# A token mixer's local kernels, made in four strips of 32 output partitions

## The chip, the cores and the metric

The kernel runs on one core of one Trainium2 chip. The metric is the device time of one execution in microseconds (us). Three runs of the kernel before gave a median of 2519.0 us, from 2516.42 to 2520.09.

## The reference

A two-layer decoder step over 272 prompt rows (16 meta tokens and 256 tokens) and 32 sample rows, width 2048, in fp32. Layer 0 is a gated short convolution and an MLP (2048 to 8192 to 2048, squared ReLU). Layer 1 is an S5 mixer and an MLP; a final norm closes it.

The S5 mixer has 128 groups of 16 channels, each with 64 complex states. Per group `g` it computes `h[t] = abar*h[t-1] + bbar u[t]` and `y[t] = Re(C h[t]) + D u[t]`, with `abar` and `bbar` made from the weights (`lambda`, `log_step`, `B`). The kernel works on four time steps at once: within a block of four, `y` gets a lower-triangular set of small matrices, the local kernels `K[g][tau] = Re(C abar^tau bbar)` (16 x 16 for tau = 0 to 3), with `D` added on the diagonal of tau = 0; what comes from earlier blocks goes through the state.

## The kernel before

**The weight stream.** All big matrices are read in slots of 256 rows by 512 columns (512 KB). SyncE issues the slots' DMAs (line 55) into four raw buffers; ScalarE makes a rounded copy `whi` (L66), VectorE the rest `wlo` (L68), three buffers of each. `WeightStream.take` makes the split two slots ahead of the one in use, and issues the DMAs for up to four slots beyond these. One slot is one *step* of `group`: 24 matmuls (L196 to L198: `whi` by high part, `whi` by low part, `wlo` by high part). Four PSUM tiles of seven belong to a group of steps; their evictions (L735 to L736, L797, L839 to L841) are put in between the matmuls on VectorE and ScalarE.

**The background list.** The S5 mixer's coefficients don't depend on the activations. They are computed during the first MLP by the list `bg`, one entry per step at the end of the step (a generator takes several steps, `None` is a step without work):

```python
            if bg:
                f = bg[0]
                ...
                        it = f()
```

Nothing but this list orders the entries against the steps. On GpSimd, which has little else to do there, they run in the order of the list as soon as what they wait for is done.

**The part that is changed.** `t_a4` turns two tables and `D` from [group, ...] to [..., group] by transposes into one PSUM tile `px` (there is one such buffer) and copies `D` as [16 channels, 128 groups]. `t_kalloc` writes zeros over the DRAM tensor `d_t` (2 MB). `t_kload(c)` loads B and C tables for 16 groups, `t_kmm(c, part)` multiplies eight groups (contraction over 128 state rows, 16 output channels by 4 x 16 columns each) into PSUM partitions 0 to 15, and ScalarE copies the result (16 x 512) into `ks`, a [16 channels, 128 groups, 4, 16] area in SBUF. `t_d` adds `D` with two GpSimd operations over 16 partitions by 2048 elements (L699, L701), and `t_tout(j)` stores from there to `d_t` the 4-j taps of input row j, one DMA of GpSimd's queue for each of four j (L704). The list after that is empty, and GpSimd's next instruction is the clearing of the S5 mixer's work area (L887), which reuses the same memory. The mixer reads `d_t` much later (`load_t`).

Of the kernel before, what the change touches and what calls it, by code (L numbers as in the profile page):

```python
# [11 lines left out]
AF = mybir.ActivationFunctionType  # L12
ALU = mybir.AluOpType
# [3 lines left out]
P = 128  # L17
# [62 lines left out]
def build(ctx, tc, I, O, dbg=None):  # L80
    nc = tc.nc
    V, S, G, T = nc.vector, nc.scalar, nc.gpsimd, nc.tensor
# [9 lines left out]
    def psum():  # L92
        return pp.tile([P, 512], F32, tag="ps", name="ps", bufs=7)

    def psum1():
        return pp.tile([P, 512], F32, tag="px", name="px", bufs=1)
# [61 lines left out]
    pend = []  # L158
# [77 lines left out]
    ident = cp.tile([P, P], F32, name="ident")  # L236
# [31 lines left out]
    big = rp.tile([P, 12000], F32, tag="BIG", name="big")  # L268
# [176 lines left out]
    d_t = dp.tile([4, 16, P, 4, 16], F32, name="d_t")  # L445

    def prep_tasks():
        L = []
        st = {}
# [7 lines left out]
        def nat(i, n=64):  # L457
            return st["vy"][:, i * 64:i * 64 + n]
# [101 lines left out]
        def t_a4():  # L560
            ps = psum1()
            for ri in range(2):
                T.transpose(out=ps[:64, ri * P:(ri + 1) * P], in_=nat(14 + ri), identity=ident)
            T.transpose(out=ps[:16, 256:256 + P], in_=nat(30, 16), identity=ident)
            V.tensor_copy(out=nat(28, P)[:16], in_=ps[:16, 256:256 + P])
            for g2 in range(2):
                sl = slice(g2 * 64, g2 * 64 + 64)
                re = ps[:64, 0:P].rearrange("p (q g) -> p q g", g=2)[:, :, g2]
                im = ps[:64, P:2 * P].rearrange("p (q g) -> p q g", g=2)[:, :, g2]
                V.tensor_copy(out=a4[sl, 0, :], in_=re)  # L570
                V.tensor_copy(out=a4[sl, 1, :], in_=re)
                V.tensor_scalar(out=a4[sl, 2, :], in0=im, scalar1=-1.0, scalar2=None, op0=ALU.mult)
                V.tensor_copy(out=a4[sl, 3, :], in_=im)
# [98 lines left out]
        def kld(c):  # L672
            off = (c % 2) * 1280
            b = st["big"]
            return (b[:, off:off + 256].rearrange("r (g c) -> r g c", g=16),
                    b[:, off + 256:off + 1280].rearrange("r (g x) -> r g x", g=16))

        def t_kload(c):
            wl, cl = kld(c)
            gs = slice(c * 16, c * 16 + 16)  # L680
            G.dma_start(out=wl, in_=d_b.rearrange("r p g c -> (r p) g c")[:, gs, :])
            G.dma_start(out=cl, in_=d_c.rearrange("r p g t c -> (r p) g (t c)")[:, gs, :])

        def ks():
            return st["big"][:16, 2560:2560 + 8192].rearrange("r (g t e) -> r g t e", t=4, e=16)

        def t_kmm(c, part):
            wl, cl = kld(c)
            ps = psum1()
            for g in range(part * 8, part * 8 + 8):  # L690
                T.matmul(out=ps[:16, g % 8 * 64:(g % 8 + 1) * 64], lhsT=wl[:, g, :], rhs=cl[:, g, :],
                         start=True, stop=True)
            g0 = c * 16 + part * 8
            pend.append(lambda: S.activation(out=ks()[:, g0:g0 + 8].rearrange("r g t e -> r (g t e)"), in_=ps[:16, :512],
                                             func=AF.Copy))

        def t_d():
            tmp = st["big"][:16, 0:2048].rearrange("r (g e) -> r g e", e=16)
            G.tensor_tensor(out=tmp, in0=ident[:16, :16].unsqueeze(1).to_broadcast([16, P, 16]),  # L699
                            in1=nat(28, P)[:16].unsqueeze(2).to_broadcast([16, P, 16]), op=ALU.mult)  # L700
            G.tensor_tensor(out=ks()[:, :, 0, :], in0=ks()[:, :, 0, :], in1=tmp, op=ALU.add)  # L701

        def t_tout(j):
            G.dma_start(out=d_t[j, :, :, j:4, :].rearrange("c g i e -> c g (i e)"),  # L704
                        in_=ks()[:, :, 0:4 - j, :].rearrange("c g t e -> c g (t e)"))

        L.append(t_kalloc)
        L += [lambda: t_kload(0), lambda: t_kload(1)]
        L += [None] * 12
        for c in range(8):  # L710
            for part in range(2):
                L.append(lambda c=c, part=part: t_kmm(c, part))
            if c < 6:
                L.append(lambda c=c: t_kload(c + 2))
            L += [None] * 4
        L += [t_d, None]
        for j in range(4):
            L += [lambda j=j: t_tout(j), None]
# [9 lines left out]
    def rhs_of(x):  # L728
        return lambda kt: (x[:, 0, kt, :], x[:, 1, kt, :])

    def rhs_hid(b):
        return lambda kt: (b[kt // 8][:, 0, kt % 8, :], b[kt // 8][:, 1, kt % 8, :])
# [42 lines left out]
    for mg in range(4):  # L775
        for part in range(3):
            if mg == 0 and part == 0:
                later(rstd_conv, 7)
            ps = group(KALL, rhs_of(xs), N0, fast=mg == 0 and part == 0)
            if mg % 2 == 0 and part == 2:  # L780
                z[mg // 2] = rp.tile([P, 2, 8, N0], F32R, tag="HID", name="z", bufs=2)
            for i in range(4):
                t = mg * 4 + i
# [40 lines left out]
    for mg in range(4):  # L824
        ps = group(KALL, rhs_hid(z), N0)
# [267 lines left out]
    def advance(n):  # L1093

        for _ in range(n):
            next(scan1, None)
# [76 lines left out]
    heavy[0] = False  # L1173
    W.limit = end0
    bg += [None] * BGOFF + prep_tasks()
    mlp(lambda: xs_mlp, N0, MLP, ssm_pre)
    assert not bg
# [4 lines left out]
    ps = psum()  # L1182
# [54 lines left out]
    part = ssm["part"]  # L1237
# [15 lines left out]
    for gi in range(NPHASE1):  # L1253
        ps = group(K1, rhs_g, N1, 0, each=lambda: advance(PUNITS))
# [55 lines left out]
    for gi, (n, mg) in enumerate(glu):  # L1310
# [3 lines left out]
        ps = group(K2 if gi < NPHASE1 else KALL, rhs_g, N1)  # L1314
# [33 lines left out]
    for mg in range(4):  # L1348
        for j in range(4):
            ps = psum()  # L1350
            for i in range(4):
                t = mg * 4 + i
                T.transpose(out=ps[:NL, i * P:(i + 1) * P], in_=xf[:, t * N1 + j * NL:t * N1 + (j + 1) * NL], identity=ident)  # L1353
            dst = ov[:, j, mg * 512:(mg + 1) * 512]
# [34 lines left out]
```

## Time and profile before

| | |
|---|---|
| median of three runs | 2519.0 us (2516.42 to 2520.09) |
| the profiled execution's own time | 2517.89 us |
| its span, first to last instruction | 2516.1 us |
| TensorE (PE) busy | 2448.6 us, 97% |
| VectorE (DVE), ScalarE (ACT), GpSimd (POOL) busy | 59%, 39%, 8% |
[...]
| DMA traffic | 418.17 MB, 166 GB/s |

1.8 us of the profiled execution's time lie outside its span. Matmuls are pipelined: a matmul of a step is recorded with 0.30 us, but they start about 0.14 us apart, so time lost on TensorE is read from the starts and from marked idle times, not from the busy share.

### The profile page before, as it was taken

The page shows a single profiled execution, that of the slowest core. Times are in us where ns is not written, and L with a number is a line of the kernel's source. Part 1 is how long each engine was busy: PE and PEld are TensorE (multiplying, and loading weights), DVE is VectorE, ACT ScalarE, POOL GpSimd, SP SyncE. Part 2 cuts the span into 40 slices and gives each one's busy share as a digit, 9 for nine tenths or more (in the row PEclk, how much of TensorE's full clock was granted, in tenths as well). Part 3 has the DMA queues.
Part 4 walks back from the last instruction along what each step waited for, and adds up shares of the span by engine and source line. Part 5 has one row for each costly group of instructions (what it writes and reads, how often), then busy time and mean ns, then how long its engine had stood idle before and what let it go on. Part 6 is the DMA issues. An engine that isn't in the chain of part 4 may idle for free. (4 is left out here: it accounts for less than half of the span.)

```text
span 2516.1 us, 43317 instructions
## 1 busy us (share of the span) xinstructions
PE 2448.6 (97%) x18078; PEld 2427.3 (96%) x18078; DVE 1477.3 (59%) x2123; ACT 974.2 (39%) x1235; POOL 189.0 (8%) x325
## 2 busy tenths in 40 slices
PE   6999999999999999999999889999999999999998
PEld 6999999999999999999998789999999999999998
DVE  5644555678565776554546964656555555545555
ACT  4333334433443333333324534443333333333334
POOL 2000000000010122000234022000000000000000
PEclk9999999999999999999999999999999999999999
DMA  6555555556666677655569544555555555555553
GB/s 153 156 157 158 158 159 175 156 158 162 191 172 206 184 218 221 192 168 169 138 167 179 149 126 144 167 163 166 168 167 163 167 165 169 161 169 166 167 168 105
DMA packets 256353, 418.17 MB, mean 166 GB/s; under 512 B 64484, under 2 KB 68260, under 8 KB 255980
## 3 DMA queue, kind: packets, MB, share of 16 engines
q1 hardware_dynamic: 248448, 389.62, 52.5%
q0 software_dynamic: 7648, 25.73, 4.9%
q8 instruction: 142, 2.33, 0.4%
q14 instruction: 55, 0.45, 0.1%
q10 hardware_dynamic: 60, 0.05, 0.0%
HBM read 392.71 MB, written 22.63 MB: 165 GB/s over the span
## 5 line engine op out<-in xcount | busy, mean ns | idle before, releaser
L68 DVE TENSOR_TENSOR wlo<-raw,whi 128x1024 fp32r<-128x1024 f32 x701 | 862.0, 1230 | 888.5 <-ACT whi L66 886.2
L66 ACT ACTIVATE whi<-raw 128x1024 fp32r<-128x1024 f32 x704 | 743.5, 1057 | 1015.0 <-PE ps L197 874.9
L196 PE MATMUL ps<-hid,whi 128*128 128x304 f32 (+1 forms) x2048 | 612.0, 299 | 11.7 <-DVE h L797 11.7
L197 PE MATMUL ps<-hid,whi 128*128 128x304 f32 (+1 forms) x2048 | 611.8, 299 | 0.0
L198 PE MATMUL ps<-xs_m,wlo 128*128 128x304 f32 (+1 forms) x2048 | 610.8, 298 | 0.1
L198 PE MATMUL ps<-hid,wlo 128*128 128x304 f32 (+1 forms) x2048 | 610.9, 298 | 0.0
L197 PE MATMUL ps<-xs_m,whi 128*128 128x304 f32 (+1 forms) x2048 | 610.2, 298 | 0.0
L196 PE MATMUL ps<-xs_m,whi 128*128 128x304 f32 (+1 forms) x2048 | 610.1, 298 | 0.0
L196 PEld LDWEIGHTS ps<-hid,whi 128*128 128x128 f32 x2048 | 385.8, 188 | 13.4 <-DVE h L797 12.7
L198 PEld LDWEIGHTS ps<-hid,wlo 128*128 128x128 f32 x2048 | 386.6, 189 | 0.0
L197 PEld LDWEIGHTS ps<-hid,whi 128*128 128x128 f32 x2048 | 385.8, 188 | 0.0
L196 PEld LDWEIGHTS ps<-xs_m,whi 128*128 128x128 f32 x2048 | 384.6, 188 | 1.1
L198 PEld LDWEIGHTS ps<-xs_m,wlo 128*128 128x128 f32 x2048 | 384.7, 188 | 0.4 <-DVE wlo L68 0.4
L197 PEld LDWEIGHTS ps<-xs_m,whi 128*128 128x128 f32 x2048 | 384.5, 188 | 0.1
L196 PE MATMUL ps<-xs,whi 128*128 128x304 f32 x768 | 233.7, 304 | 3.5 <-DVE h L388 3.5
L198 PE MATMUL ps<-xs,wlo 128*128 128x304 f32 x768 | 233.4, 304 | 0.0
L197 PE MATMUL ps<-xs,whi 128*128 128x304 f32 x768 | 232.9, 303 | 0.0
L735 ACT ACTIVATE hid<-at 128x304 fp32r<-128x304 f32 (+1 forms) x128 | 57.8, 452 | 293.0 <-DVE at L841 293.0
L198 PE MATMUL ps<-g,wlo 128*128 128x288 f32 x512 | 151.1, 295 | 0.0
L196 PE MATMUL ps<-g,whi 128*128 128x288 f32 x512 | 151.1, 295 | 0.0
L197 PE MATMUL ps<-g,whi 128*128 128x288 f32 x512 | 150.7, 294 | 0.0
L196 PEld LDWEIGHTS ps<-xs,whi 128*128 128x128 f32 x768 | 145.9, 190 | 3.8 <-DVE h L388 3.7
(283 smaller groups left out, 2337.9 us busy)
## 6 DMA issues: line engine op xcount, KB each, us to landing
raw<-in_mlp_w_up SPq DMA_DIRECT2D x256, 512.0 KB, 3.7
raw<-in_mlp_w_down SPq DMA_DIRECT2D x256, 512.0 KB, 3.7
raw<-in_conv_w_in SPq DMA_DIRECT2D x96, 512.0 KB, 3.7
raw<-in_conv_w_out SPq DMA_DIRECT2D x32, 512.0 KB, 3.6
raw<-in_ssm_glu_w_b SPq DMA_DIRECT2D x32, 512.0 KB, 3.7
raw<-in_ssm_glu_w_a SPq DMA_DIRECT2D x32, 512.0 KB, 3.5
ssm_big<-d_m SPq DMA_DIRECT2D x64, 128.0 KB, 3.4
d_m<-prep POOLq DMA_DIRECT2D x16, 256.0 KB, 9.4
```

Of the source, the lines that this page charges most:

```text
L66: self.nc.scalar.activation(out=hi, in_=r, func=AF.Copy)
L68: eng.tensor_tensor(out=lo, in0=r, in1=hi.bitcast(F32), op=ALU.subtract)
L196: T.matmul(out=o, lhsT=wh, rhs=xh, start=si == 0 and kk == 0, stop=False)
L197: T.matmul(out=o, lhsT=wh, rhs=xl, start=False, stop=False)
L198: T.matmul(out=o, lhsT=wl, rhs=xh, start=False, stop=si + 2 >= len(kts) and kk == 1)
L735: S.activation(out=dh, in_=src, func=AF.Copy)
```

## The change

`t_kmm` handles all 16 groups of a `t_kload` in one call. Group `g = 4x + s` of the sixteen goes to PSUM partitions 32x to 32x + 31 (four strips), columns 64s to 64s + 63. Its stationary operand is read 32 columns wide: its own 16 and the following 16, whose rows of output nobody uses. One ScalarE copy (128 x 256) then serves 16 groups. `ks` becomes [128, 32 x 4 x 16], in which a strip holds 16 channels of every fourth run of four groups. `t_d` works on 128 partitions by 512 elements; for this `t_a4` brings `D` into the strips with four small matmuls against the identity, each followed by a VectorE copy of the strip's columns and a copy of a 16 x 16 identity (before: one transpose, one copy). `t_tout(j)` issues four DMAs, one per strip, so sixteen instead of four. The number of entries in the list is unchanged: where the second call of `t_kmm` stood is a `None`.

```diff
-            T.transpose(out=ps[:16, 256:256 + P], in_=nat(30, 16), identity=ident)
-            V.tensor_copy(out=nat(28, P)[:16], in_=ps[:16, 256:256 + P])
+            V.memset(nat(28, P), 0.0)
+            for x in range(4):
+                sl = slice(32 * x, 32 * x + 16)
+                T.matmul(out=ps[sl, 256:256 + P], lhsT=nat(30, 16), rhs=ident, start=True, stop=True)
+                V.tensor_copy(out=nat(28, 32)[sl].rearrange("r (c s) -> r c s", s=4),
+                              in_=ps[sl, 256:256 + P].rearrange("r (c x s) -> r c x s", x=4, s=4)[:, :, x, :])
+                V.tensor_copy(out=nat(29, 16)[sl], in_=ident[sl, sl])
...
-            return st["big"][:16, 2560:2560 + 8192].rearrange("r (g t e) -> r g t e", t=4, e=16)
+            return st["big"][:, 2560:2560 + 2048].rearrange("r (g t e) -> r g t e", t=4, e=16)
...
-        def t_kmm(c, part):
+        def t_kmm(c):
             wl, cl = kld(c)
+            wf = st["big"][:, (c % 2) * 1280:(c % 2) * 1280 + 272]
             ps = psum1()
-            for g in range(part * 8, part * 8 + 8):
-                T.matmul(out=ps[:16, g % 8 * 64:(g % 8 + 1) * 64], lhsT=wl[:, g, :], rhs=cl[:, g, :],
-                         start=True, stop=True)
-            g0 = c * 16 + part * 8
-            pend.append(lambda: S.activation(out=ks()[:, g0:g0 + 8].rearrange("r g t e -> r (g t e)"), in_=ps[:16, :512],
-                                             func=AF.Copy))
+            for s_ in range(4):
+                for x in range(4):
+                    g = x * 4 + s_
+                    T.matmul(out=ps[32 * x:32 * x + 32, s_ * 64:(s_ + 1) * 64], lhsT=wf[:, g * 16:g * 16 + 32],
+                             rhs=cl[:, g, :], start=True, stop=True)
+            pend.append(lambda: S.activation(out=ks()[:, c * 4:c * 4 + 4].rearrange("r g t e -> r (g t e)"),
+                                             in_=ps[:, :256], func=AF.Copy))
 
         def t_d():
-            tmp = st["big"][:16, 0:2048].rearrange("r (g e) -> r g e", e=16)
-            G.tensor_tensor(out=tmp, in0=ident[:16, :16].unsqueeze(1).to_broadcast([16, P, 16]),
-                            in1=nat(28, P)[:16].unsqueeze(2).to_broadcast([16, P, 16]), op=ALU.mult)
+            tmp = st["big"][:, 0:512].rearrange("r (g e) -> r g e", e=16)
+            G.tensor_tensor(out=tmp, in0=nat(29, 16).unsqueeze(1).to_broadcast([P, 32, 16]),
+                            in1=nat(28, 32).unsqueeze(2).to_broadcast([P, 32, 16]), op=ALU.mult)
             G.tensor_tensor(out=ks()[:, :, 0, :], in0=ks()[:, :, 0, :], in1=tmp, op=ALU.add)
 
         def t_tout(j):
-            G.dma_start(out=d_t[j, :, :, j:4, :].rearrange("c g i e -> c g (i e)"),
-                        in_=ks()[:, :, 0:4 - j, :].rearrange("c g t e -> c g (t e)"))
+            dst = d_t[j].rearrange("c (k x s) i e -> c x k s (i e)", x=4, s=4)
+            for x in range(4):
+                G.dma_start(out=dst[:, x, :, :, j * 16:],
+                            in_=ks()[32 * x:32 * x + 16, :, 0:4 - j, :].rearrange("r (k s) t e -> r k s (t e)", s=4))
...
         for c in range(8):
-            for part in range(2):
-                L.append(lambda c=c, part=part: t_kmm(c, part))
+            L.append(lambda c=c: t_kmm(c))
             if c < 6:
                 L.append(lambda c=c: t_kload(c + 2))
-            L += [None] * 4
+            L += [None] * 5
```

## Rows read from the trace of the kernel before

**Rows 1.** The page's busy times: engine, us, share of the span, instructions.
```profile
PE 2448.6 (97%) x18078; PEld 2427.3 (96%) x18078; DVE 1477.3 (59%) x2123; ACT 974.2 (39%) x1235; POOL 189.0 (8%) x325
```

**Rows 2.** The chain that ended last: start, us, what. Its beginning, and after the MLP.
```profile
1254.63 17.71 DMA raw<-in_mlp_w_down
...
1273.53 1.23 DVE wlo L68
...
1337.52 3.59 DMA d_u<-h
```

**Rows 3.** TensorE in order of time, around its two stops: start, duration, [idle before].
```profile
1251.23 0.30 PE L198 MATMUL ps<-hid,wlo 128*128 128x304 f32 x1
1255.04 0.42 PE L196 MATMUL ps<-hid,whi 128*128 128x304 f32 x1 [3.51 <-DVE h L797]
...
1269.86 0.30 PE L198 MATMUL ps<-hid,wlo 128*128 128x304 f32 x1
1275.19 0.62 PE L196 MATMUL ps<-hid,whi 128*128 128x304 f32 x1 [5.04 <-DVE h L797]
```

**Rows 4.** Two stretches, tile ps alone: PE, PEld, DVE, ACT busy, PEclk, DMA.
```profile
1242.10:1280.30 38.20, 29.64 (x186) 29.16 (x187) 3.71 (x8) 0.00 (x0) 0.87 0.77 141
1285.00:1325.00 40.00, 40.00 (x291) 40.00 (x290) 5.54 (x12) 0.00 (x0) 1.00 0.61 169
```

**Rows 5.** GpSimd in order of time, 1238 to 1285 us.
```profile
1242.27 3.69 POOL L699 TENSOR_TENSOR prep<-ident,nat 16x2048 f32<-16x2048 f32 x1 [46.77 <-PE px L691]
1246.03 5.54 POOL L701 TENSOR_TENSOR prep<-prep 16x2048 f32<-16x2048 f32 x1
1251.87 0.53 POOL L704 DMA_DIRECT2D d_t<-prep  x1 [0.30 <-POOL prep L701]
...
1274.66 4.37 POOL L887 MEMSET ssm_big<- 128x5120 f32 x1 [18.40 <-DMA d_t<-prep]
```

**Rows 6.** VectorE in order of time, same stretch.
```profile
1243.79 3.26 DVE L68 TENSOR_TENSOR wlo<-raw,whi 128x1024 fp32r<-128x1024 f32 x1 [1.40 <-ACT whi L66]
...
1247.46 4.45 DVE L841 SCALAR_TENSOR_TENSOR at<-zt 128x304 f32<-128x304 f32 x1
...
1254.52 0.46 DVE L797 TENSOR_TENSOR h<-h,ps 128x304 f32<-128x304 f32 x1
```

**Rows 7.** GpSimd's DMA queue (packets, MB, share of 16 engines): 1249 to 1255, 1249 to 1277, 648 to 675 us.
```profile
q0 software_dynamic: 16, 0.52, 82.6%
...
q0 software_dynamic: 272, 1.31, 63.0%
...
q0 software_dynamic: 640, 2.10, 38.4%
```

**Rows 8.** One line's DMAs, the four stores L704 of t_tout: time to landing.
```profile
DMA to landing us min/median/max: 6.9/14.2/19.4
```

**Rows 9.** TensorE in order of time around one call of t_kmm.
```profile
1236.36 0.30 PE L198 MATMUL ps<-hid,wlo 128*128 128x304 f32 x1
1236.59 1.07 PE L691 MATMUL px<-prep 128*16 128x64 f32 x16
1237.59 0.40 PE L196 MATMUL ps<-hid,whi 128*128 128x304 f32 x1
```

**Rows 10.** One line's matmul: t_kmm's form, duration min/median/max ns, first and last start.
```profile
L691 PE MATMUL px<-prep x256: 219/219/230, 1060.1 to 1242.0; 128*16 128x64 f32 x128
```

**Rows 11.** TensorE, then VectorE, in order of time during t_a4.
```profile
594.74 0.27 PE L564 MATMUL px<-ident,nat 128*16 128x128 f32 x1
...
595.05 0.28 DVE L565 COPY nat<-px 16x128 f32<-16x128 f32 x1 [1.05 <-PE px L564]
595.26 0.20 DVE L570 COPY a<-px 64x64 f32<-64x64 f32 x1
```

**Rows 12.** GpSimd's groups by line and form: count, busy us, mean ns.
```profile
L654 POOL DMA_DIRECT2D d_m<-prep x32 | 20.0, 632 | 22.6 <-DVE prep L645 19.9 <-DMA d_c<-prep 2.4 <-issue 0.2
...
L1107 POOL TENSOR_TENSOR ssm_xr<-a,ssm_big 128x320 f32<-128x320 f32 x2 | 1.8, 886 | 0.1
```

## The prediction

> **What bounds the kernel now.** First the busy times: TensorE is busy 97% of the span, the others far less [rows 1]. So what matters is where TensorE stops, what work goes through it, and what feeds it. A step takes 24 matmuls; undisturbed, 291 matmuls of the steps start in 40.00 us, 0.137 us apart [rows 4].
>
> Next the chain that ended last. It begins at 1254.63 us, in the middle of the kernel, with a weight slot's DMA that took 17.71 us [rows 2]; behind the MLP it goes on through the stores that start the S5 mixer [rows 2]. So up to 1254 us TensorE has lost hardly anything to waits, and what is gained around there comes off the end.
>
> Then TensorE in order of time around that place. It stops twice: its matmuls start at 1251.23 and then at 1255.04, and at 1269.86 and then at 1275.19, both times until a VectorE eviction [rows 3]. In the stretch that holds both, 1242.10 to 1280.30, it started 186 matmuls at a mean granted clock of 0.87; undisturbed these take 186 x 40.00/291 = 25.6 us, and the stretch has 38.2. **12.6 us are lost there:** 3.7 + 5.2 in the two holes (each distance of starts less 0.14), and the other 3.7 in matmuls at the lower clock behind them [rows 3, 4].
>
> Last, who caused it, in the other engines' order of time. GpSimd runs the two operations of `t_d`, 3.69 and 5.54 us over 16 partitions, from 1242.27 to 1251.6 [rows 5]. In that time a VectorE subtraction L68 took 3.26 us (1.23 in the chain [rows 2]) and L841 took 4.45, where another operation of 128x304 takes 0.46 [rows 6]: VectorE was held for 2.0 + 4.0 = 6.0 us. TensorE's hole was 3.7, so about 2.3 us of lateness were covered by work done ahead. Then come the four stores: the last landed 19.4 us after its issue [rows 8], and GpSimd's clearing L887 waited 18.40 us for them [rows 5]. This is when the weight slot took 17.71 us: the second hole.
>
> **The change part by part.**
>
> *GpSimd's two operations (`t_d`).* From 2048 elements per partition to 512. A quarter of the rows is 0.92 and 1.38 us [rows 5]; by GpSimd's 128x320 multiplication, 0.886 us [rows 12], 512 elements take 1.4. So 2.3 to 2.8 us instead of 9.2. VectorE was held for 6.0 of 9.2 us; of 2.8 it is held for at most 2.8, likely 1.8, against the 2.3 us of cover: a hole of 0 to 0.5 us, and I take 0. (If VectorE's work ahead were used up just then, the loss would be the whole 1.8.) The scratch of the multiplication now lies over an earlier call's table only, so it may run some steps earlier; both operations are then apart, which helps. The first hole with its slow clock goes.
>
> *The stores (`t_tout`).* The bytes stay: 1.31 MB. The first of before was 16 packets, one of 32 KB for each DMA engine, and held all sixteen for 82.6% of 6 us, 5.0 us at 106 GB/s [rows 7]. All four held them for 63.0% of 28 us, 17.6 us in 272 packets, 17 per engine [rows 7]. The weight slot that came through in 17.71 us needs 16 packets per engine if one moves a 2 KB row: one weight packet to each packet of a store, as if the two queues took turns. This is my reading of why the slot was late: not the bytes, but long packets. The mixer's earlier stores show how short pieces are packed: 2.10 MB in 640 packets, that is eight DMAs of 16 KB per engine in 4 packets of 4 KB and a small one [rows 7]. By that, the strips' DMAs have per engine 2, 2, 1 and 1 packets of data (8, 6, 4, 2 KB for j = 0 to 3) and a small one, times four strips: 40 packets instead of 17. With the engine time unchanged at 17.6 us (16 partitions per DMA as before), and 40 weight packets of about 0.1 us between, the stores last some 21 us and let 2.5 slots pass instead of one. TensorE ran 18.0 us from the first store's issue until it was empty [rows 3, 5]. The first slot lands after 16 of 40 turns, 8 to 11 us; the split and the wait for it take 3 more: in time. The second lands at 17 to 20 us and is wanted at 18.0 + 3.3 - 3 = 18.3. I take a hole of 0.6 us, with bounds of 0 and the old 5.2 + 1.9 us (if the turns are not the cause, and the engine time alone is). GpSimd issues sixteen DMAs, 16 x 0.63 = 10 us by the nearest row [rows 12], less than the transfer, with nothing behind them but L887. L887 starts when they have landed; `t_d` begins some 3 us earlier (the last products come with the call that was the pair's first) and is 6.5 us shorter, so it starts earlier than before even if the stores last 21 us.
>
> [...]
>
> *The products (`t_kmm`).* 128 groups as before, and 256 passes (two matmul records per group). A call took 1237.59 - 1236.36 - 0.14 = 1.09 us for 16 passes [rows 9]; I put it at 16 x 0.054 + 0.22 for entering and leaving. Eight calls of 32 passes fewer by eight entries: 8 x 0.22 = **-1.8 us**. Does a stationary operand of 32 columns, written to another strip each time, keep 0.054 us a pass? The trace of before has all outputs at partition 0. Bounds: above, each pass takes the 0.219 us that one lasts from start to end [rows 10], +42 us; below, four strips run beside each other. A matmul of 304 columns comes every 0.137 us and one of 64 every 0.054, so a column costs 0.35 ns and 64 of them 0.022 us; a quarter of that saves 0.017 us x 256 = -4.4 us. I take 0.054: the records are the same kind and the pass was already mostly not columns.
>
> *ScalarE.* Eight copies of 128x256 for sixteen of 16x512: less, and ScalarE is busy 39% [rows 1]. Nothing; if the cover were gone, still a gain.
>
> *`D` into strips (`t_a4`).* One transpose goes, four small matmuls come, each into the PSUM tile that VectorE then reads. Before, no matmul follows a read of the same tile. If each waits for the copy ahead of it, a round is the matmul 0.27, hand-over 0.04, copy 0.20 [rows 11], back to TensorE 0.06 (VectorE's L797 ends at 1254.98, TensorE starts at 1255.04 [rows 3, 6]): 0.57. Three rounds and a last short matmul: **+1.8 us**. Bounds: 0.3 without waits, 3.4 with the identity's copies in the round. TensorE has nothing else in its queue to run meanwhile; the eight copies and a memset run on VectorE inside these stops, and it had waited 1.05 us for TensorE there [rows 11].
>
> [...]
>
> *Sum:* -12.6 + 0.6 - 1.8 + 1.8 = **-12.0 us**. Against the profiled execution's own 2517.9 us that is 2505.9. That execution lies 1.1 us below the median of the runs, so the median after should be some 2506 to 2507: I say **2506.5**.
>
> **The rivals.**
>
> *The stores still starve the stream.* If the DMA engines' 17.6 us count and not the length of the packets, the second hole and its clock stay in part or whole: up to 7.1 us back, 2507 to 2513; if sixteen transfers also last 3 us longer than four, 2516. For it: the same 16 partitions feed each DMA. Against: one slot in 17.7 us fits the turns.
>
> *A new wait takes the gain.* GpSimd's operations again fall on a full VectorE, or `t_a4`'s rounds are 2 us each: 5 to 8 us back, 2512 to 2516 and no change that can be told.
>
> *The strips run beside each other:* 4.4 us more, 2502. [...] Against it: a pass is mostly fixed time.
>
> *The other side: the strips drain the array.* If a change of strip costs a pass its full length, +42 us: 2548. It decides the sign from 12.0/256 = 0.047 us per pass on, and is measurably slower from 17/256 = 0.066. For it: no row with an output off partition 0. Against: the same form of matmul, pipelined to a quarter of its length.
>
> **How the numbers follow.** 0.2% of the median is 5.0 us, about what a measurement of this kernel can tell from no change: faster means below 2514, slower above 2524. Chances: forecast (2504 to 2510) 0.58; starved stream 0.18, half of it below 2514; new wait 0.08, nearly all "same"; strips beside each other 0.09; drain 0.07, nearly all slower. Faster 0.58 + 0.09 + 0.10 = 0.77, same 0.16, slower 0.07. The drain and a few per cent at the ends are left out of the range: 2501 to 2517.
>
> **What would show it.** Right: no TensorE idle above 1 us and a clock of 1.00 in the 45 us after the last product; L68 and L841 there near 1.2 and 0.5 us; no weight slot's DMA above 12 us; products at 1.9 to 2.0 us a call; the chain no longer begins with a slot of the MLP near 1250; three stops of 0.2 to 0.4 us in `t_a4`. Wrong: a hole behind the stores as before, or records of the products that don't overlap.

## The result and the profile after

The kernel after takes 2495.77 us in the median of four runs (2491.91 to 2498.42); four runs of the kernel before beside it give 2517.71 (2514.84 to 2520.09). The ratio is 0.9912, with a 95% interval of 0.9895 to 0.993: 22 us less. The prediction was 2506.5 with a range from 2501, so the sign was right and the gain was 10 us larger than said. The profiled execution took 2495.24 us, with a span of 2493.4.

The page's busy times of the kernel after, to be read beside [rows 1]:

```profile
PE 2431.8 (98%) x18085; PEld 2412.8 (97%) x18085; DVE 1473.5 (59%) x2131; ACT 968.6 (39%) x1227; POOL 189.8 (8%) x337
```

TensorE is still the engine that is nearly always busy, with 16.8 us less of busy time and some of its idle time gone. Where both come from is read by finding one and the same matmul of a step (the same slot, the same term) in both traces and comparing its start:

| the same step's matmul | before, us | after, us | after less before |
|---|---|---|---|
| behind `t_a4` | 594.77 | 597.90 | +3.1 (of it +0.7 already ahead of `t_a4`) |
| just ahead of the first product call | 1059.88 | 1063.52 | +3.6 |
| behind the last product call | 1242.11 | 1233.06 | -9.1 |
| behind the two holes | 1281.25 | 1259.67 | -21.6 |
| end of the S5 mixer | 1512.89 | 1490.28 | -22.6 |

So `t_a4` costs 2.4 us, the products give 12.7, the two holes give 12.5, and nothing else moves by more than about 1 us. (Between the profiled executions' own times, 2517.89 and 2495.24, it is 22.65.)

**`t_a4`.** TensorE in order of time in the kernel after; an idle time and its releaser stand in brackets:

```profile
595.27 0.38 PE L563 MATMUL px<-ident,nat 128*64 128x128 f32 x2
595.58 0.39 PE L568 MATMUL px<-ident,nat 128*16 128x128 f32 x2
596.24 0.39 PE L568 MATMUL px<-ident,nat 128*16 128x128 f32 x2 [0.27 <-DVE nat L569]
596.91 0.39 PE L568 MATMUL px<-ident,nat 128*16 128x128 f32 x2 [0.28 <-DVE nat L569]
597.58 0.39 PE L568 MATMUL px<-ident,nat 128*16 128x128 f32 x2 [0.28 <-DVE nat L569]
597.90 0.41 PE L196 MATMUL ps<-hid,whi 128*128 128x304 f32 x1
```

Each matmul of `D` from the second on waits for VectorE's copy out of the strip ahead of it: three stops, in rounds of 0.67 us.

**The products.** TensorE in order of time around the last call of the kernel after, beside [rows 9]:

```profile
1228.79 0.30 PE L198 MATMUL ps<-hid,wlo 128*128 128x304 f32 x1
1229.03 0.65 PE L701 MATMUL px<-prep 128*32 128x64 f32 x32
1229.61 0.41 PE L196 MATMUL ps<-hid,whi 128*128 128x304 f32 x1
```

Thirty-two passes and their call cost 1229.61 - 1228.79 - 0.14 = 0.68 us, where sixteen cost 1.09 before. One pass still lasts 219 ns from start to end, as in [rows 10]; what changed is the distance of starts, on the mean (0.65 - 0.22)/31 = 0.014 us, against (1.07 - 0.22)/15 = 0.057 before.

**The two holes.** GpSimd, then VectorE, in order of time in the kernel after, beside [rows 5, 6]:

```profile
1209.05 1.06 POOL L708 TENSOR_TENSOR prep<-nat 128x512 f32<-128x512 f32 x1 [22.84 <-PE px L701]
1230.27 1.31 POOL L710 TENSOR_TENSOR prep<-prep 128x512 f32<-128x512 f32 x1 [20.17 <-ACT prep L703]
1231.88 7.35 POOL L715 DMA_DIRECT2D d_t<-prep  x11 [0.30 <-POOL prep L710]
...
1252.01 4.39 POOL L897 MEMSET ssm_big<- 128x5120 f32 x1 [6.06 <-DMA d_t<-prep]
...
1231.11 1.55 DVE L68 TENSOR_TENSOR wlo<-raw,whi 128x1024 fp32r<-128x1024 f32 x1 [0.97 <-ACT whi L66]
...
1233.08 0.47 DVE L851 SCALAR_TENSOR_TENSOR at<-zt 128x304 f32<-128x304 f32 x1
```

The two operations of `t_d` are now 21 us apart and take 1.06 and 1.31 us instead of 3.69 and 5.54. The subtraction L68 beside the second one takes 1.55 us, where it had taken 3.26; L851, which was L841 before, takes 0.47 instead of 4.45. `ssm_big`'s clearing waits 6.06 us for the stores instead of 18.40.

Stretches of the kernel after (PE, PEld, DVE, ACT and POOL busy, granted clock, DMA share, GB/s), then the DMA queues from 1229 to 1261 us (packets, MB, share of 16 engines), beside [rows 4, 7]; the last line is the weights' queue of the kernel before, from 1249 to 1277 us:

```profile
1230.00:1235.00 5.00, 5.00 (x39) 5.00 (x38) 3.02 (x5) 2.49 (x4) 4.43 (x7) 1.00 0.62 122
...
1245.00:1250.00 5.00, 5.00 (x39) 5.00 (x38) 2.45 (x4) 1.15 (x2) 0.74 (x1) 1.00 0.83 262
...
sum 45.00, PE 45.00 PEld 45.00 DVE 24.13 ACT 15.58 POOL 17.74; mean PE 5.00 PEld 5.00 DVE 2.68 ACT 1.73 POOL 1.97
...
q1 hardware_dynamic: 2570, 4.97, 47.0%
q0 software_dynamic: 640, 1.31, 27.2%
...
q1 hardware_dynamic: 1330, 2.57, 25.4%
```

In the 45 us from 1230 on TensorE has no idle time, at a clock of 1.00 in every stretch. The stores are 40 packets per engine (640/16), as predicted, but they hold the engines for 27.2% of 32 us, 8.7 us, and not for 17.6. The weights' queue moves 4.97 MB in these 32 us, 155 GB/s; in the 28 us around the stores of before it moved 2.57 MB, 92 GB/s. The chain that ended last now begins at 914.12 us instead of 1254.63.

### The profile page after: what moved, and what is told of

It reads as the page before. It is cut to its first block, busy times and chain, and to the rows that moved or that the text cites. A ratio compares the mean times of both kernels' runs of the same rounds, so it can differ in the third digit from the quotient of the medians.

```text
span 2493.4 us, 43347 instructions
## 1 busy us (share of the span) xinstructions
PE 2431.8 (98%) x18085; PEld 2412.8 (97%) x18085; DVE 1473.5 (59%) x2131; ACT 968.6 (39%) x1227; POOL 189.8 (8%) x337
## 4 chain that ended last, share of the span: by engine, by line
PE 61%; issue 1%; DMA 1%; POOL 0%; DVE 0%; ACT 0%; SPq 0%; DVEq 0%; POOLq 0%; ACTq 0%
PE ps L196 19%; PE ps L198 19%; PE ps L197 19%; PE ps L1134 1%; PE ps L982 1%; PE ps L1125 1%; DMA ssm_big<-d_m 1%; PE ps L1363 0%; PE ps L1001 0%; PE px L701 0%; PE ps L1150 0%; POOL ssm_big L1120 0%; POOL ssm_xr L1119 0%; ACT sq L321 0%; DVE h L807 0%
## 5 line engine op out<-in xcount | busy, mean ns | idle before, releaser
L68 DVE TENSOR_TENSOR wlo<-raw,whi 128x1024 fp32r<-128x1024 f32 x701 | 860.3, 1228 | 869.2 <-ACT whi L66 868.7
L66 ACT ACTIVATE whi<-raw 128x1024 fp32r<-128x1024 f32 x704 | 743.8, 1057 | 1023.5 <-PE ps L197 894.9
```

The costliest lines, as they stand in the source:

```text
L66: self.nc.scalar.activation(out=hi, in_=r, func=AF.Copy)
L68: eng.tensor_tensor(out=lo, in0=r, in1=hi.bitcast(F32), op=ALU.subtract)
```

## The experiments

Eleven kernels ran. The mean spacing of passes is always worked out as above: the length of the call's group, less 0.22 for its last pass, over the other passes.

**The change's three parts, each alone.** First the strips: the kernel before with the products written to four strips, sixteen groups in one call, and four copies by ScalarE that bring each strip back to partitions 0 to 15, so that `D` and the stores stay as they were.

```diff
-            for g in range(part * 8, part * 8 + 8):
-                T.matmul(out=ps[:16, g % 8 * 64:(g % 8 + 1) * 64], lhsT=wl[:, g, :], rhs=cl[:, g, :], ...)
+            for s_ in range(4):
+                for x in range(4):
+                    g = x * 4 + s_
+                    T.matmul(out=ps[32 * x:32 * x + 32, s_ * 64:(s_ + 1) * 64], lhsT=wf[:, g * 16:g * 16 + 32], ...)
...
+                for x in range(4):
+                    S.activation(out=ks()[:, g0:g0 + 4]..., in_=ps[32 * x:32 * x + 16, :256], func=AF.Copy)
```

> The kernel before with the products alone in strips: sixteen groups a call into four strips as in the changed kernel, but ScalarE brings each strip back to partitions 0 to 15 with four copies of 16x256, so the two GpSimd operations over 16x2048 and the four stores are those of before. Theory A: 16 x 1.09 us become 8 x 0.68 us, 12 us less, about 2506 us, and both holes of TensorE behind the products are still there (3.7 and 5.2 us with the lower clock behind them). Theory C (the products were hidden, and the 22 us come from the stores and GpSimd alone): no change, 2518 us.

2503.98 us (2503.37 to 2506.27), a ratio of 0.9954 [0.9939, 0.9969]. TensorE in order of time, one call and the two holes:

```profile
1227.02 0.65 PE L696 MATMUL px<-prep 128*32 128x64 f32 x32
...
1239.12 0.41 PE L196 MATMUL ps<-hid,whi 128*128 128x304 f32 x1 [1.26 <-ACT whi L66]
...
1259.22 0.62 PE L196 MATMUL ps<-hid,whi 128*128 128x304 f32 x1 [3.77 <-ACT whi L66]
```

The call is that of the kernel after. From the first call to the last the same matmul moves by -12.7 us against before: the whole gain of the products comes with the strips, without the new store layout. Both holes are still there, each shorter than in [rows 3] and now ended by a ScalarE copy L66; why shorter isn't settled.

Then `t_d` alone: the kernel before without its two GpSimd operations (`D` is left out).

```diff
         def t_d():
-            tmp = ...
-            G.tensor_tensor(out=tmp, ...)
-            G.tensor_tensor(out=ks()[:, :, 0, :], ...)
+            return
```

> The kernel before without the two GpSimd operations that add D (D is left out of the local kernels, 9.2 us of GpSimd are gone). Theory F (these hold VectorE's two-input operations, and that is the first hole): L68 and L841 stay at 1.2 and 0.5 us, the first hole of 3.7 us and the 1.7 us lost at the lower clock behind it go, the second hole stays at about 5 us: 2512 us. Rival: the first hole has another cause, it stays, 2518 us.

2509.06 us (2506.76 to 2510.65), a ratio of 0.9973 [0.9962, 0.9984]. The first hole is gone, no VectorE operation around it takes more than 1.3 us, and the second hole stays, at 3.06 us instead of 5.04; why it is shorter isn't settled. TensorE in order of time:

```profile
1268.27 0.62 PE L196 MATMUL ps<-hid,whi 128*128 128x304 f32 x1 [3.06 <-DVE h L794]
```

So the first hole was GpSimd's, and the second has another cause.

Then the stores alone: each store of before cut into four by groups, from the same 16 partitions.

```diff
-            G.dma_start(out=d_t[j, :, :, j:4, :]..., in_=ks()[:, :, 0:4 - j, :]...)
+            for x in range(4):
+                q = slice(32 * x, 32 * x + 32)
+                G.dma_start(out=d_t[j, :, q, j:4, :]..., in_=ks()[:, q, 0:4 - j, :]...)
```

> The kernel before with each of the four stores cut into four by ranges of 32 groups: sixteen DMAs, but all from partitions 0 to 15. Theory D (the prediction's: it is the length of the packets that keeps the weight stream waiting, the two queues take turns): packets per engine rise from 17 to some 36 to 40, engine time stays near 17.6 us, the second hole of TensorE shrinks to under 1.5 us, 2510 to 2512 us. Theory E (the strips lie at other partitions, so more ways out of SBUF are used, and that halved the engine time from 17.6 to 8.7 us): the engine time stays at 17 to 18 us and the second hole stays at 4 us or more, 2516 to 2518 us. If the engine time falls to some 9 us here too, the partitions have no part in it.

2513.67 us (2508.32 to 2515.85), a ratio of 0.9983 [0.9974, 0.9993]. TensorE around the two places, GpSimd from the first store to the clearing, then GpSimd's DMA queue from 1250 to 1282 us:

```profile
1256.26 0.41 PE L196 MATMUL ps<-hid,whi 128*128 128x304 f32 x1 [3.49 <-DVE h L799]
...
1272.01 0.41 PE L196 MATMUL ps<-hid,whi 128*128 128x304 f32 x1 [0.63 <-DVE h L799]
...
1253.08 5.87 POOL L706 DMA_DIRECT2D d_t<-prep  x10 [0.29 <-POOL prep L701]
...
1275.98 4.37 POOL L889 MEMSET ssm_big<- 128x5120 f32 x1 [8.15 <-DMA d_t<-prep]
...
q0 software_dynamic: 576, 1.31, 53.8%
```

Both DMA queues in the 16 us from the first store's first packet on, before (1253 to 1269 us) and here (1254.2 to 1270.2 us):

```profile
q0 software_dynamic: 204, 1.05, 86.5%
q1 hardware_dynamic: 189, 0.39, 6.3%
...
q0 software_dynamic: 423, 1.14, 86.6%
q1 hardware_dynamic: 389, 0.76, 12.4%
```

The first hole stays at 3.49 us. The second falls from 5.04 to 0.63, with 0.28 and 0.71 in two places near it. The engines are held as long as before, 53.8% of 32 us or 17.2 us, in 36 packets each instead of 17, and from the first store's issue to the clearing it takes 22.9 us, as 22.8 before [rows 5]. But in the first 16 us the weights' queue moves 0.76 MB beside them instead of 0.39. So the length of the pieces starved the stream, not the engine time; and more packets, 36 for 17, didn't shorten the engine time here. One difference is left beside the length: from the eleventh store on GpSimd waits 0.3 to 1.2 us for an earlier store ahead of each issue. What that is worth no run separates.

The three parts alone give 11.6, 6.8 and 4.3 us by their ratios, 22.7 together; the change gave 22. Each interval reaches some 2 to 4 us to either side, and `t_a4`'s cost is in none of the three.

**What in the strips makes a pass cheap.** The kernel after, with only the order of the loops changed, strip by strip:

```diff
-            for s_ in range(4):
-                for x in range(4):
+            for x in range(4):
+                for s_ in range(4):
```

> The changed kernel with the sixteen products of a call in another order: all four of one strip, then the next strip, instead of one strip after the other in turn. Everything else is the same. Theory A (passes that go to different strips run beside each other in TensorE, and that is why a call of 32 passes takes 0.68 us): neighbours in the same strip can't overlap so, a call goes back to 32 x 0.054 + 0.22 = 1.95 us or near it, eight calls 10 us more, about 2506 us. Theory B (the gain of the products comes from half as many calls, or from the stationary operand of 32 columns): the order doesn't matter, a call stays at 0.68 us and the time at 2496 us.

2499.8 us (2499.03 to 2504.36), a ratio of 0.994 [0.9924, 0.9957]. TensorE, the last call and the matmul behind it:

```profile
1235.35 1.39 PE L701 MATMUL px<-prep 128*32 128x64 f32 x32
1236.67 0.41 PE L196 MATMUL ps<-hid,whi 128*128 128x304 f32 x1
```

A call takes 0.7 us longer, 5.9 over the eight. The order matters, so the number of columns or of calls is not what saved this time. But 0.038 us a pass lies between the two theories' numbers; where it comes from is read below, from the starts of the single passes.

Then 32 columns, all into one strip: the kernel before with a wider operand.

```diff
+            wf = st["big"][:, (c % 2) * 1280:(c % 2) * 1280 + 272]
...
-                T.matmul(out=ps[:16, ...], lhsT=wl[:, g, :], rhs=cl[:, g, :],
+                T.matmul(out=ps[:32, ...], lhsT=wf[:, g * 16:g * 16 + 32], rhs=cl[:, g, :],
```

> The kernel before, with the stationary operand of the products 32 columns wide as in the changed kernel, but everything still in partitions 0 to 31 and eight groups a call. The products strip by strip took (1.39 - 0.22)/31 = 0.038 us from pass to pass, those of before (1.07 - 0.22)/15 = 0.057. Theory W (the width or the full strip makes a pass shorter): 16 passes take 0.8 us instead of 1.07. Theory A (only a change of strip does): 1.07 us as before, and the 0.038 of the run strip by strip is then from the places where the strip changes.

One execution took 2519.81 us, within the runs of before beside it (2514.32 to 2520.13). A call on TensorE:

```profile
1218.51 1.08 PE L692 MATMUL px<-prep 128*32 128x64 f32 x16
```

(1.08 - 0.22)/15 = 0.057 us: the width plays no part. The same in partitions 32 to 63, from where ScalarE then copies:

```diff
-                T.matmul(out=ps[:32, ...
+                T.matmul(out=ps[32:64, ...
```

> The kernel before with 32-column stationary operands, eight groups a call, all in the second strip (partitions 32 to 63). In the run strip by strip a pass took 0.038 us on the mean though only three of 31 passes of a call change the strip; in strip 0 alone it takes 0.057. Theory A (only changes of strip make passes overlap): 16 passes take 1.07 us here too. Rival: strips beside the first are faster in themselves, 16 passes take 0.8 us or less.

One execution took 2515.24 us beside 2515.49 of before; the call again takes 1.08 us, 0.057 a pass. Which strip it is plays no part either.

Then narrow operands in four strips: the strips alone, with 16 columns.

```diff
-                    T.matmul(out=ps[32 * x:32 * x + 32, ...], lhsT=wf[:, g * 16:g * 16 + 32], ...)
+                    T.matmul(out=ps[32 * x:32 * x + 16, ...], lhsT=wl[:, g, :], ...)
```

> The kernel with the products alone in strips, but with stationary operands of 16 columns, written to 16 partitions of each strip. Theory A (the strips run beside each other): 32 passes in 0.65 us as with 32 columns. Theory W (the width is part of it): 0.9 us or more.

One execution took 2504.3 us; a call of 32 passes takes 0.64 us, as with 32 columns. The strips are what counts.

And two strips in turn, in the kernel after:

```diff
-            for s_ in range(4):
-                for x in range(4):
-                    g = x * 4 + s_
+            for g in (0, 4, 1, 5, 2, 6, 3, 7, 8, 12, 9, 13, 10, 14, 11, 15):
+                for x, s_ in (divmod(g, 4),):
```

> The changed kernel with the products in turn over two strips only: eight groups between strips 0 and 1, then eight between strips 2 and 3. Theory A with a strip as the thing that is occupied: a pass starts as soon as its own strip is free, so two strips give half of the single strip's 0.038 to 0.057 us, 0.019 to 0.028 us a pass, a call's 32 passes 0.8 to 1.1 us: between the 0.65 of four and the 1.39 of one. If any change of strip is enough and the number does not matter: 0.65.

One execution took 2494.95 us, within the runs of the kernel after. A call on TensorE:

```profile
1209.48 0.90 PE L700 MATMUL px<-prep 128*32 128x64 f32 x32
```

(0.90 - 0.22)/31 = 0.022 us. In a row:

| passes written to | us from one start to the next, on the mean |
|---|---|
| one strip (16 or 32 columns, first or second strip) | 0.057 |
| four strips, one strip after another | 0.038 |
| two strips in turn | 0.022 |
| four strips in turn | 0.014 |

These means hide one distance that is the same in all. The count behind the PE time says how many passes of a call have started by the end of a stretch. The kernel after, then strip by strip (granted clock, DMA share and GB/s behind it):

```profile
1229.00:1229.05 0.05, 0.03 (x4) 1.00 0.00 0
1229.00:1229.10 0.10, 0.07 (x4) 1.00 0.00 0
1229.00:1229.13 0.13, 0.10 (x8) 1.00 0.00 0
1229.00:1229.16 0.16, 0.14 (x8) 1.00 0.00 0
1229.00:1229.19 0.19, 0.17 (x12) 1.00 0.00 0
...
1235.30:1235.59 0.29, 0.24 (x4) 1.00 0.00 0
1235.30:1235.60 0.30, 0.25 (x5) 1.00 0.00 0
1235.30:1235.61 0.31, 0.26 (x6) 1.00 0.00 0
```

With four strips in turn the passes come in fours: four start 0.006 to 0.007 us apart, then none until the next four, 0.056 us behind the four ahead of them (0.080 once, behind the first). In one strip, before, single passes start 0.056 apart. Strip by strip, the fifth pass starts 0.248 us behind the first and the sixth 0.006 behind the fifth: the trace's starts then read as two rows, each with 0.056 us between its passes, so the second strip begins when the first has had five of its eight passes. With a strip beginning 0.253 us behind the one ahead of it and lasting 0.415 to its last start, (3 x 0.253 + 0.415)/31 = 0.038. Two strips in turn give pairs 0.056 us apart, and the second two strips begin 0.26 us behind the first two: 0.022. So in each of these runs a strip takes a pass every 0.056 us, and the order decides how many strips run at once. Why the next strip begins only after five passes is open.

**The stops in `t_a4`.** The kernel after, with the four matmuls of `D` ahead of all copies:

```diff
                 T.matmul(out=ps[sl, 256:256 + P], lhsT=nat(30, 16), rhs=ident, start=True, stop=True)
+            for x in range(4):
+                sl = slice(32 * x, 32 * x + 16)
                 V.tensor_copy(out=nat(28, 32)[sl]...
```

> The changed kernel with the four small matmuls of D ahead of the first copy out of their tile, nothing else. Theory G (three rounds of matmul, hand-over and copy cost 2.5 us in the changed kernel because each matmul waits for the copy ahead of it): TensorE's three stops of 0.27 us there go, and the place costs 0.5 us or less against the kernel before, 2 us less than in the changed kernel: 2493.7 us, which a comparison of runs can hardly tell from 2495.8, the trace can. Rival: the four fp32 matmuls themselves cost the 2.5 us: no stop is left but the place takes as long.

TensorE in order of time:

```profile
596.99 0.41 PE L568 MATMUL px<-ident,nat 128*16 128x128 f32 x8
597.33 0.41 PE L196 MATMUL ps<-hid,whi 128*128 128x304 f32 x1
```

The three stops are gone, and the place costs 0.4 us against before instead of 2.4. The runs, 2493.46 us (2492.24 to 2500.28), a ratio of 0.9916 [0.9902, 0.9929], can't tell it from the kernel after.

**Why the stores hold the engines for half the time.** The kernel after, with the same sixteen stores in another order: first all four of strip 0, then of strips 1, 2 and 3.

```diff
-        def t_tout(j):
-            dst = d_t[j].rearrange("c (k x s) i e -> c x k s (i e)", x=4, s=4)
-            for x in range(4):
+        def t_tout(x):
+            for j in range(4):
+                dst = d_t[j].rearrange("c (k x s) i e -> c x k s (i e)", x=4, s=4)
```

> The changed kernel with its sixteen stores in another order: the four of strip 0, then those of strip 1, 2 and 3, so the order over (j, strip) is turned round. Theory P (the engine time fell from 17.2 to 8.7 us because stores of strips that lie at other ways out of SBUF are in flight together): neighbours in the queue now share the same partitions, the engine time rises to 14 to 17 us; TensorE has no hole of over 1 us all the same, since the packets are short. Rival: it is the pieces or the sixteen DMAs themselves, engine time 8 to 9 us as before.

And in the order 0, 2, 1, 3 within each `j`:

```diff
-            for x in range(4):
+            for x in (0, 2, 1, 3):
```

> The changed kernel with the stores of each j in the order of strips 0, 2, 1, 3 instead of 0, 1, 2, 3. If strips 0 and 1 share their ways out of SBUF and 2 and 3 theirs, neighbours in the queue are now always at different ones, and the engine time falls below 8.7 us (7 to 8); if each strip has its own, it stays at 8.7. TensorE sees no difference: 2495 us.

One execution each took 2496.63 and 2494.03 us, both within the runs of the kernel after. GpSimd's DMA queue from 1229 to 1261 us, strip after strip:

```profile
q0 software_dynamic: 640, 1.31, 47.5%
```

and in the order 0, 2, 1, 3:

```profile
q0 software_dynamic: 640, 1.31, 20.5%
```

Same bytes, same 640 packets: 15.2, 8.7 (after) and 6.6 us of engine time by the order alone. Of the fifteen steps from a store to the next, one, seven and all fifteen lead from partitions below 64 to partitions above or back; with the stores in pieces, all from partitions 0 to 15, none did, at 17.2 us. In the kernel after every step changes the strip too, as in the order 0, 2, 1, 3, so between these two, 8.7 and 6.6 us, only the changes of half differ; whether strip 0 beside strip 1 gains anything by itself no run separates. TensorE has no idle time in the stretch in the order 0, 2, 1, 3. Strip after strip it has one:

```profile
1257.52 0.41 PE L196 MATMUL ps<-hid,whi 128*128 128x304 f32 x1 [0.93 <-DVE h L807]
```

So a rest of the second hole comes back at 15.2 us of engine time; at 8.7 and at 6.6 us TensorE has none, and the order is worth nothing there.

## Why the prediction was wrong by half of the gain

**The step that failed is the products' term, -1.8 us: it measured -12.7.** The prediction divided a pass into a column part that strips could share (0.022 us) and a fixed rest that they couldn't, because "the pass was already mostly not columns". The rows of before held no evidence for the second half of that: 0.057 us between two passes into one strip doesn't tell what a pass into another strip waits for. The runs showed that a strip takes a pass every 0.056 us, fixed rest included, and that four strips do so side by side: 0.014 us a pass on the mean. The calls' lengths give 16 x 1.09 - 8 x 0.68 = 12.0 of the 12.7 us: the eight entries fewer are 8 x 0.22 = 1.8 of it, as forecast, and the closer passes the other 10.2; where the last 0.7 lies isn't settled. The rival "the strips run beside each other" was thus the right mechanism, at a chance of 0.09 and with a price of 4.4 us that left out the fixed part; so the range, which was made from it, ended at 2501. By the whole distance shared among four, its lower bound would have been 256 x 0.054 x 3/4 = 10.4 us beside the 1.8. Measured, passes to four strips in turn start 0.057/0.014 = 4.1 times as close as passes to one. The experiments with one strip, two and four in turn, and 16 columns show that it is the turn among strips, not the width. What a pass into the same strip waits for they don't show.

**The holes: right,** -12.5 for -12.6 + 0.6. The cause of the first (GpSimd's operations holding VectorE) was shown by leaving them out. That of the second (long packets, as if the queues took turns) was shown as far as the length goes: pieces alone, at the same engine time, took the hole from 5.04 to 0.63 us and let 0.76 MB of weights through in the first 16 us instead of 0.39. That the queues take strict turns isn't shown. The residue of 0.6 was forecast from the unchanged engine time: the kernels that hold the engines for 17.2 and 15.2 us have 0.63 (with 0.28 and 0.71 near it) and 0.93; in the kernel after it doesn't come, as the engines are held for 8.7 us only. GpSimd's sizes (0.92 to 1.4 us each, apart) came as said.

**The stores' engine time: wrong, without consequence.** "Unchanged at 17.6 us" measured 8.7. That the stores last "some 21 us" came near all the same, 20.1 us from the first issue to the clearing, but with less than half the engine time: by luck. I took the limit to be 16 partitions per DMA. Every store of these runs reads 16 partitions, and yet the sixteen held the engines for 17.2 us with all of them from partitions 0 to 15, for 15.2 us strip by strip, for 6.6 us when every store is followed by one from the other half, and for 8.7 us in between, where seven of fifteen are. What lies behind this order no run shows; the "ways out of SBUF" of the expectations are an assumption of mine.

**`t_a4`: right in kind, 2.4 instead of 1.8.** The stops of 0.27 to 0.28 us lie in the "0.2 to 0.4" forecast; a round is 0.67 instead of 0.57, because the matmul of `D` is two passes (0.39 us) and was costed as one record (0.27).

**What would show it.** All signs named for "right" came but one: the products take 0.7 us a call and not 1.9 to 2.0. (L68 took 1.55 us once; of the weight slots whose landing the trace has, the slowest took 9.1 us.) Both named for "wrong" stayed away. The rivals of the starved stream, the new wait and the drained array didn't happen.

## What to carry to other kernels

Small products like these, with 16 or 32 output columns, should go to the four 32-partition strips of PSUM in turn, neighbouring matmuls to different strips: here the passes then started 0.014 us apart on the mean instead of 0.057, so the fixed part was shared too. A store that runs beside a stream should be cut into short pieces: with 36 packets per engine instead of 17 the weights' queue moved 0.76 MB in 16 us instead of 0.39. GpSimd operations like the two of `t_d` should be spread over all partitions: 1.06 and 1.31 us instead of 3.69 and 5.54, beside which VectorE's L68 and L841 took 3.26 and 4.45 us instead of 1.23 and 0.47. Where several matmuls fill parts of one PSUM tile, put all of them ahead of the first copy out of it: `t_a4` then cost 0.4 us instead of 2.4.

## What was not expected of the hardware

Passes of the same kind started 0.057, 0.038, 0.022 or 0.014 us apart on the mean by nothing but the strips that they write and their order, while each strip took one every 0.056 us and a pass lasted 219 ns from start to end in the median, before as after. Beside stores that held the DMA engines for the same 17 us, another queue moved 0.76 MB in 16 us instead of 0.39 when their packets were cut shorter. Sixteen stores of the same 1.31 MB held the DMA engines for 15.2, 8.7 or 6.6 us by nothing but their order.
